# Turning the delta rule's v and output on VectorE and through DRAM instead of on TensorE

## The chip, the cores and the metric

The program runs on one core of one Trainium2 chip. The metric is the device time of that core in microseconds: the median of several executions, and beside it one execution that was taken with the hardware profiler. The names of the engines are those of the profile: PE is TensorE's matrix multiply and PEld its weight load, DVE is VectorE, ACT is ScalarE, POOL is GpSimd, SP is SyncE.

## The reference

One decoder layer on 256 tokens of width 2048. Branch A, which the change touches, is a gated delta rule with 8 heads of width 128, worked in chunks of 64 tokens; branch B is attention; a gated feed-forward layer follows. Cut to branch A:

```python
qkv = silu(causal_dwconv(qkv, conv_w))             # width 4, per channel
q, k = l2norm(q), l2norm(k)                        # v is not normed
t_mat = triangular_solve(eye + a_mat, eye)         # per head and chunk of 64
u = t_mat @ (v * beta)
w = t_mat @ (kb * exp(gc))
def step(state, ...):                              # over the 4 chunks
    v_new = u_n - w_n @ state
    o = qg_n @ state + qk_n @ v_new
    state = state * gl_n + kd_n.T @ v_new
o = rms_norm(o, norm_w) * silu(z)                  # per token and head, over the 128 channels
```

The input projection gives all of its results with channels as rows and tokens as columns. The delta rule needs v the other way round (tokens of a chunk as rows), and its output has to be turned back (channels as rows) for the projection behind it. These two turns are what the change is about.

## The kernel before, in words

All matrix products with weights run on PE with tokens as columns. Each float32 weight block of 1 MB is fetched by SP into one of four buffers, split into a high part (ACT, line 110) and a low part (DVE, line 107), and multiplied in three passes of 128x256 (line 100, through `main_mm`). A block takes two splits of 128x1024 on each of ACT and DVE, and 48 matmuls; high and low parts have two buffers each. A `chunk` (line 181) is two such blocks that fill one of three PSUM buffers, and `join` (line 198) scales it into SBUF and so frees the buffer.

The order of the work: four groups (two heads each) of the chunks q, k, v and z come first, then four groups of the attention's q and k with two long v products, then 16 gate chunks, the branch projections, the output projection, the feed-forward layer. Beside this stream of weight products the small work of the delta rule is written as a Python generator, `gdn` (line 441), one for each group. `main_mm` counts a cost for each matmul and at 1700, that is after 16 matmuls of 128x256, calls `tick`, which moves each open generator forward to its next `yield`. A group of four chunks is 24 ticks; a generator has 51 ticks, so the next two generators begin while it still runs (24 and 48 ticks later).

That order is only a priority. The instructions of every engine are put into their queues by a scheduler at build time: it simulates the program, and an instruction goes out when its engine is free, its data is there and its tile has a place, the one traced earliest first. Instructions can thus run far ahead of the place at which they were written. Each queue is then fixed, and each engine works through its queue in order, waiting where data is late.

A tile belongs to a pool and has a tag (its name, if none is given). All tiles of a tag share `bufs` places. In pool `g`, which the delta rule uses, most have `bufs=1`: `kq` (q and k after the convolution, for PE), `un` (the joined chunk that the convolution reads), `kqh` and `kql` (the high and low parts of `kq`, line 461), `sqq` and `so` (squares, both with tag `sq`, lines 444 and 612), `v`, `vt`, `X`, `E`, `u`, `ot`. A new tile of a tag takes the place once all readers and writers of the former tile in that place are done.

What a generator does, in its order: squares of q; Gram products `g0`, `g1` (lines 467 to 471) from `kqh` and `kql`; norms and decays into `st`, `rt2`, `aq0`, `aq1`; v turned by four PE transposes into PSUM and scaled by `rt2` on DVE into `vb` (lines 496 to 502); the blocks of the triangular matrix sent through DRAM by POOL (`dA`, `dC`, `Xa`); after ten ticks, 15 steps of substitution on DVE (`X`); more DRAM trips on POOL's queue (`dX`, `dE`, `E`, `UB`); from tick 34 on small PE products (`py`, `pu`, `w0`, `z0`, `w1`, `r1`), which read `vb`; the output `po` in PSUM. Then ACT copies `po` to `ot` (line 611) and squares it with a row sum (line 614), a root and a reciprocal give `st[:, 7]`, DVE scales `ot` (line 618), and after seven ticks four PE transposes (line 623) turn it into PSUM, from where DVE multiplies it into `ya` (line 625). The small PSUM tiles of all this share five places (`sdt`).

v's convolution (`conv4`, line 412) writes its result over a rearranged view, so that a head pair of one chunk is one 128x128 block (line 643).

The `g` pool is closed in the third attention group (line 741), and the gate tile `gts` of the next pool takes over its memory.

Of the kernel before, what the change touches and what calls it, by code (L numbers as in the profile page):

```python
# [19 lines left out]
P = 128  # L20
# [52 lines left out]
def layer_kernel(ctx: ExitStack, tc: tile.TileContext, xT, pos, cst, vec, convw, ffw, bdv,  # L73
# [8 lines left out]
    def r3(t, b):  # L82
        return t.rearrange("p (a b) -> p a b", b=b)
# [87 lines left out]
    def sdt(name):  # L171
        return pst[1].tile([P, 512], F32, name=name, tag="sd")
# [239 lines left out]
    def conv4(t, ps, b0, to=None):  # L412
        un = g.tile([P, 2, T], F32, name="un", bufs=1)
        join(un, ps, R1b)
        for j in range(2):
            w = cwv[:, b0 + j, :]
            act.activation(t[:, j, :], un[:, j, :], AF.Identity, scale=w[:, 3:4])
            for d in (1, 2, 3):
                dve.scalar_tensor_tensor(t[:, j, d:], un[:, j, :T - d], w[:, 3 - d:4 - d], t[:, j, d:],
                                         op0=ALU.mult, op1=ALU.add)  # L420
        if to is None:
            act.activation(t, t, AF.Silu)
        else:
            act.activation(to, t.rearrange("p j (b c) -> p j b c", c=64), AF.Silu)
# [12 lines left out]
    def wait(n):  # L437
        for _ in range(n):
            yield

    def gdn(h0, kq, v):
# [54 lines left out]
        pvt = r3(sdt("pvt"), P)  # L496
        for i in range(2):
            for b in range(2):
                pe.transpose(pvt[:, 2 * i + b, :], v[:, 2 * i + b, :], ident)
        vb = g.tile([P, 2, 2, P], F32, name="vb")  # L500
        dve.tensor_tensor(vb, pvt.rearrange("p (i b) d -> p i b d", b=2), rt2[:, :, :, None].to_broadcast([P, 2, 2, P]),
                          op=ALU.mult)
# [10 lines left out]
        pool.tensor_copy(X, C["rows"])  # L513
        yield from wait(10)
# [3 lines left out]
        for i in range(1, 16):  # L518
            tm = g.tile([P, 2, 2, 16], F32, name="tm", tag="tm", bufs=1)
            dve.tensor_tensor(tm[:, :, :, :i + 1], Xd[:, :, :, :i + 1],  # L520
                              Ad[:, :, None, :i + 1, i].to_broadcast([P, 2, 2, i + 1]), op=ALU.mult)
            dve.tensor_reduce(Xd[:, :, :, i], tm[:, :, :, :i + 1], axis=AX.X, op=ALU.add, negate=True)
            if i % 4 == 3:
                yield
        X0, Xm, X1 = Xd[:, 0, :, :16], r3(X[:, :64], 32)[:, :, 16:], Xd[:, 1, :, :16]
# [84 lines left out]
        ot = g.tile([P, 4, P], F32, name="ot", bufs=1)  # L610
        act.copy(ot, po)
        so = g.tile([P, 4, P], F32, name="so", tag="sq", bufs=1)
        for p in range(4):
            act.activation(so[:, p], ot[:, p], AF.Square, accum_out=st[:, 4, p:p + 1])
# [3 lines left out]
        dve.tensor_tensor(ot, ot, st[:, 7, :, None].to_broadcast([P, 4, P]), op=ALU.mult)  # L618
        yield from wait(7)
        pot = r3(sdt("pot"), T)  # L620
        for i in range(2):
            for j in range(2):
                pe.transpose(pot[:, j, i * P:(i + 1) * P], ot[:, 2 * i + j, :], ident)
        yv = ya[:, h0:h0 + 2, :]
        dve.scalar_tensor_tensor(yv, pot, gnv, yv, op0=ALU.mult, op1=ALU.mult)
# [4 lines left out]
    for gr in range(4):  # L630
        h0 = 2 * gr
        kq = g.tile([P, 2, 2, T], F32, name="kq", bufs=1)
        v = g.tile([P, 4, 2 * 64], F32, name="v", bufs=1)
        vt = g.tile([P, 2, T], F32, name="vt", bufs=1)
        for a, t in enumerate((kq[:, 1], kq[:, 0], vt)):
# [4 lines left out]
            if a < 2:  # L640
                conv4(t, ps, 8 * a + h0)
            else:
                conv4(t, ps, 8 * a + h0,
                      v.rearrange("p b (j c) -> p j b c", c=64))
# [320 lines left out]
```

## Time and profile before

| what | value |
|---|---|
| time, median of 3 runs | 1455.61 us (1451.09 to 1455.78) |
| the profiled execution's own time | 1450.71 us |
| its span, first to last instruction | 1448.9 us |
| mean granted TensorE clock | 0.998 |
| busy PE, DVE, ACT, POOL | 1437.9, 951.5, 741.1, 158.1 us |

The delta rule runs from 49.7 us (the first squares of q, line 445) to 355.6 us (the last product into `ya`, line 625). Busy shares over the whole span say little about it, since more than two thirds of the span have other work; the stretches of it are read one by one in the prediction. A busy PE is not a PE at its peak, as the ends of matmuls are modelled: the number of matmuls that start in a stretch is the better measure.

### The profile page before, as it was taken

To read this page: it belongs to the slowest core of one execution; us is meant where nothing else is said; L and a number is where in the kernel's file an instruction comes from. 1 tells how busy PE (TensorE), PEld (TensorE's weight loads), DVE (VectorE), ACT (ScalarE), POOL (GpSimd) and SP (SyncE) were. 2 spreads that over 40 slices of the span, in tenths; PEclk is the share of its full clock that TensorE was granted. 3 is DMA by queue.
4 is the path that set the end of the run, shared out by engine and by line. 5 is a ranking of instruction groups with operands and counts; after the bars stand their busy time and mean duration, and the time that the engine had idled before them with its cause. 6 is when DMAs were issued, how large, how long until landed. Compare 5 with 4: busy or idle time off the path is not lost.

```text
span 1448.9 us, 26704 instructions
## 1 busy us (share of the span) xinstructions
PE 1437.9 (99%) x11232; PEld 1381.6 (95%) x11232; DVE 951.5 (66%) x1389; ACT 741.1 (51%) x1052; POOL 158.1 (11%) x237
## 2 busy tenths in 40 slices
PE   9999999999999999999999999999999999999997
PEld 8999999999999999999999999999999998888886
DVE  7889887765654546767776666666666666555454
ACT  5675774446553444444554545445455455444444
POOL 0024133230030000101120000000000000000000
PEclk9999999999999999999999999999999999999999
DMA  9466656545455555566585555555555555555552
GB/s 342 150 204 211 202 183 210 191 162 173 161 196 180 201 195 187 201 213 226 202 268 197 201 183 199 202 182 199 195 188 200 195 187 202 189 189 203 187 191 88
DMA packets 47465, 283.79 MB, mean 196 GB/s; under 512 B 7744, under 2 KB 8912, under 8 KB 15216
## 3 DMA queue, kind: packets, MB, share of 16 engines
q1 hardware_dynamic: 40352, 270.37, 53.7%
q0 software_dynamic: 6272, 9.61, 2.6%
q8 instruction: 88, 1.44, 0.4%
q10 hardware_dynamic: 720, 2.10, 0.4%
q14 instruction: 33, 0.27, 0.1%
HBM read 275.33 MB, written 3.82 MB: 193 GB/s over the span
## 4 chain that ended last, share of the span: by engine, by line
PE 95%; ACT 2%; DMA 1%; DVE 1%; issue 0%; SPq 0%; ACTq 0%
PE ps_up L100 33%; PE pd L88 17%; PE ps_gate L100 12%; PE ps_gdn L100 7%; PE ps_moba L100 6%; PE ps_wo L100 6%; PE ps_br L100 6%; PE ps_v L100 3%; PE ps_z L100 2%; DMA wraw<-in_w_gdn 1%; PE g L88 1%; DVE wl L107 0%; ACT wh L110 0%; PE ps_bd L88 0%; PE po L88 0%
## 5 line engine op out<-in xcount | busy, mean ns | idle before, releaser
L107 DVE TENSOR_TENSOR wl<-wraw,wh 128x1024 fp32r<-128x1024 f32 (+1 forms) x500 | 598.9, 1235 | 185.8 <-ACT wh L110 185.2
L110 ACT CAST wh<-wraw 128x1024 fp32r<-128x1024 f32 (+1 forms) x500 | 496.6, 1041 | 416.0 <-PE ps_up L100 160.4
L100 PE MATMUL ps_up<-h,wh 128*128 128x256 f32 x2816 | 479.3, 276 | 0.0
L100 PEld LDWEIGHTS ps_up<-h,wh 128*128 128x128 f32 x2816 | 424.1, 188 | 0.1
L100 PE MATMUL ps_up<-h,wl 128*128 128x256 f32 x1408 | 388.7, 276 | 0.0
L100 PEld LDWEIGHTS ps_up<-h,wl 128*128 128x128 f32 x1408 | 264.3, 188 | 0.0
L100 PE MATMUL ps_gate<-hc,wh 128*128 128x256 f32 x1024 | 175.7, 277 | 0.0
L100 PEld LDWEIGHTS ps_gate<-hc,wh 128*128 128x128 f32 x1024 | 154.5, 188 | 0.0
L100 PE MATMUL ps_gate<-hc,wl 128*128 128x256 f32 x512 | 141.8, 277 | 0.0
L88 PE MATMUL pd<-wl,ah 128*128 128x512 f32 x336 | 129.5, 389 | 0.0
L88 PE MATMUL pd<-wh,al 128*128 128x512 f32 x336 | 129.1, 389 | 0.0
L100 PE MATMUL ps_gdn<-hc,wh 128*128 128x256 f32 x704 | 124.7, 280 | 0.0
L100 PEld LDWEIGHTS ps_gdn<-hc,wh 128*128 128x128 f32 x704 | 107.3, 188 | 0.3 <-ACT wh L110 0.3
L100 PE MATMUL ps_gdn<-hc,wl 128*128 128x256 f32 x352 | 98.2, 279 | 0.8 <-DVE wl L107 0.8
L100 PEld LDWEIGHTS ps_gate<-hc,wl 128*128 128x128 f32 x512 | 96.1, 188 | 0.1
L100 PE MATMUL ps_moba<-hc,wh 128*128 128x256 f32 x512 | 92.4, 281 | 0.0
L88 PE MATMUL pd<-wh,ah 128*128 128x512 f32 x336 | 92.1, 389 | 0.0
L200 DVE TENSOR_TENSOR unf<-ps_up,R 128x512 f32<-128x512 f32 x44 | 30.4, 692 | 89.2 <-PE ps_up L100 89.2
L100 PE MATMUL ps_wo<-mc,wh 128*128 128x256 f32 x512 | 87.1, 276 | 0.0
L839 POOL TENSOR_TENSOR acts<-sg,cvf 128x256 f32<-128x256 f32 x44 | 32.4, 737 | 439.2 <-ACT sg L838 432.1
L100 PEld LDWEIGHTS ps_moba<-hc,wh 128*128 128x128 f32 x512 | 78.7, 189 | 0.1
L100 PEld LDWEIGHTS ps_wo<-mc,wh 128*128 128x128 f32 x512 | 77.0, 188 | 0.0
(448 smaller groups left out, 1973.0 us busy)
## 6 DMA issues: line engine op xcount, KB each, us to landing
wraw<-in_w_up SPq DMA_DIRECT2D x88, 1024.0 KB, 4.8
wraw<-in_w_dn SPq DMA_DIRECT2D x44, 1024.0 KB, 4.8
wraw<-in_w_gate SPq DMA_DIRECT2D x32, 1024.0 KB, 4.9
wraw<-in_w_gdn SPq DMA_DIRECT2D x30, 1024.0 KB, 5.1
wraw<-in_w_moba SPq DMA_DIRECT2D x16, 1024.0 KB, 5.0
wraw<-in_w_o SPq DMA_DIRECT2D x16, 1024.0 KB, 4.9
wraw<-in_w_mv SPq DMA_DIRECT2D x8, 1024.0 KB, 5.0
wraw<-in_w_ba SPq DMA_DIRECT2D x8, 1024.0 KB, 4.9
```

The source lines that it names most:

```text
L88: pe.matmul(ps, a, b, start=(start and i == 0), stop=(stop and i == n - 1), **kw)
L100: pe.matmul(ps, a, b, start=start, stop=stop, skip_group_check=True)
L107: return (eng or dve).tensor_tensor(lo, src, hi.bitcast(F32), op=ALU.subtract)
L110: act.copy(hi, src)
L200: dve.tensor_tensor(dst, ps, r, op=ALU.mult)
L839: pool.tensor_tensor(acts[:, c, :], sg, t[:, 1, :], op=ALU.mult)
```

## The change

v's turn. v's convolution now writes plain `v` (`[P, 2, T]`). DVE turns each 32x32 block of it in place of the four PE transposes, into `Zv`, which has tag `kqh`. POOL writes `Zv` to a DRAM tile `dV` in four transfers of 32 partitions (512 runs of 128 bytes each, 64 KB), and reads `vb` back in two (64 partitions of 2 KB runs, 128 KB each). The scaling by `rt2` is no longer part of the eviction on DVE: ACT does it in place, in four `mul`s of 128x128, after the substitution.

The output's turn. ACT takes the squares straight from `po` in PSUM (their values go to a `jk` tile, unused), and scales `po` by `st[:, 7]` with four `mul`s into `ot`; the copy and DVE's scaling are gone. One tick later DVE turns 32x32 blocks in two instructions of 128x256 into `Zo` (tag `kqh`), POOL writes `dO` in four transfers of 512 runs of 128 bytes and reads `yT` (tag `kql`, 256 KB in 2 KB runs) back in one. Ten ticks later DVE multiplies `yT` into `ya`. The generator has 55 ticks.

```diff
+    def rows32(z, r):
+        return z[32 * r:32 * r + 32].rearrange("p c x d -> p (c x) d")
...
-        pvt = r3(sdt("pvt"), P)
-        for i in range(2):
-            for b in range(2):
-                pe.transpose(pvt[:, 2 * i + b, :], v[:, 2 * i + b, :], ident)
-        vb = g.tile([P, 2, 2, P], F32, name="vb")
-        dve.tensor_tensor(vb, pvt.rearrange("p (i b) d -> p i b d", b=2), rt2[:, :, :, None].to_broadcast([P, 2, 2, P]),
-                          op=ALU.mult)
+        Zv = g.tile([P, 2, 8, 32], F32, name="Zv", tag="kqh", bufs=1)
+        dve.transpose(Zv.rearrange("p c x d -> p x c d"), v.rearrange("p j (x c t) -> p (j x) c t", c=2, t=32))
...
+        dV = dr.tile([32, 2, 1024], F32, name="dV")
+        for r in range(4):
+            pool.dma_start(dram(dV, 32 * r, (2048, 32), (P, 16), (1, 32)), rows32(Zv, r))
+        vb = g.tile([P, 2, 2, P], F32, name="vb")
+        for j in range(2):
+            pool.dma_start(vb[64 * j:64 * j + 64].rearrange("p i b d -> p (i b d)"),
+                           dram(dV, 512 * j, (1024, 2), (2048, 32), (1, 512)))
         yield from wait(10)
...
+        for i in range(2):
+            for b in range(2):
+                act.mul(vb[:, i, b], vb[:, i, b], rt2[:, i, b:b + 1])
...
-        ot = g.tile([P, 4, P], F32, name="ot", bufs=1)
-        act.copy(ot, po)
-        so = g.tile([P, 4, P], F32, name="so", tag="sq", bufs=1)
+        jk = g.tile([P, P], F32, name="jk", bufs=1)
         for p in range(4):
-            act.activation(so[:, p], ot[:, p], AF.Square, accum_out=st[:, 4, p:p + 1])
+            act.activation(jk, po[:, p], AF.Square, accum_out=st[:, 4, p:p + 1])
...
-        dve.tensor_tensor(ot, ot, st[:, 7, :, None].to_broadcast([P, 4, P]), op=ALU.mult)
-        yield from wait(7)
-        pot = r3(sdt("pot"), T)
+        ot = g.tile([P, 4, P], F32, name="ot", bufs=1)
+        for p in range(4):
+            act.mul(ot[:, p], po[:, p], st[:, 7, p:p + 1])
+        yield
+        Zo = g.tile([P, 4, 4, 32], F32, name="Zo", tag="kqh", bufs=1)
         for i in range(2):
-            for j in range(2):
-                pe.transpose(pot[:, j, i * P:(i + 1) * P], ot[:, 2 * i + j, :], ident)
+            dve.transpose(Zo.rearrange("p r (j i) t -> p i j r t", i=2)[:, i],
+                          ot[:, 2 * i:2 * i + 2].rearrange("p x (r d) -> p x r d", d=32))
+        dO = dr.tile([32, 2048], F32, name="dO")
+        for r in range(4):
+            pool.dma_start(dram(dO, 32 * r, (2048, 32), (P, 16), (1, 32)), rows32(Zo, r))
+        yT = g.tile([P, 2, T], F32, name="yT", tag="kql", bufs=1)
+        pool.dma_start(yT.rearrange("p j t -> p (j t)"), dram(dO, 0, (512, 4), (2048, 32), (1, 512)))
+        yield from wait(10)
         yv = ya[:, h0:h0 + 2, :]
-        dve.scalar_tensor_tensor(yv, pot, gnv, yv, op0=ALU.mult, op1=ALU.mult)
+        dve.scalar_tensor_tensor(yv, yT, gnv, yv, op0=ALU.mult, op1=ALU.mult)
```

More of the change, by code (lines that the diff above doesn't have):

```diff
@@ L410, in decay, with conv4 @@
         dve.tensor_scalar(cols[:, 0:2, :].rearrange("p a b -> p (a b)"), pt[:, :32], -1.0, None, op0=ALU.mult)
-    def conv4(t, ps, b0, to=None):
+    def conv4(t, ps, b0):
         un = g.tile([P, 2, T], F32, name="un", bufs=1)
@@ L420, in conv4 @@
                                          op0=ALU.mult, op1=ALU.add)
[L421 to L424, printed above, removed]
+        act.activation(t, t, AF.Silu)
     dG = dr.tile([16, T], F32, name="dG", bufs=1)
@@ L632, in layer_kernel @@
         kq = g.tile([P, 2, 2, T], F32, name="kq", bufs=1)
-        v = g.tile([P, 4, 2 * 64], F32, name="v", bufs=1)
-        vt = g.tile([P, 2, T], F32, name="vt", bufs=1)
-        for a, t in enumerate((kq[:, 1], kq[:, 0], vt)):
+        v = g.tile([P, 2, T], F32, name="v", bufs=1)
+        for a, t in enumerate((kq[:, 1], kq[:, 0], v)):
             if gr == 0 and a < 2:
@@ L639, in layer_kernel @@
                 ps = chunk(pair(w_gdn, 4 * gr + a), hc, KD, "gdn")
[L640 to L644, printed above, removed]
+            conv4(t, ps, 8 * a + h0)
             if gr == 0 and a == 1:
```

## The prediction, on record before the result

> **What bounds the kernel now.** I read the page first (busy times, then the shares of the chain that ended last), then that chain in order of time, then stretches of 10 us, then the groups of instructions and the transfers that the change touches.
>
> ```profile
> span 1448.9 us, 26704 instructions
> PE 1437.9 (99%) x11232; PEld 1381.6 (95%) x11232; DVE 951.5 (66%) x1389; ACT 741.1 (51%) x1052; POOL 158.1 (11%) x237
> PE 95%; ACT 2%; DMA 1%; DVE 1%; issue 0%; SPq 0%; ACTq 0%
> ```
>
> The chain is PE's for 95% of the span. Modelled ends make a busy PE look full anyway, so I measure its pace by counts. The chain in order of time (start, length, what, how many):
>
> ```profile
> 183.28 0.44 PE pot L623 x4
> 184.51 2.19 PE g L88 x12
> 187.74 0.44 PE pvt L499 x4
> ...
> 212.31 1.14 PE ps_moba L100 x10
> ...
> 368.04 1.86 PE ps_gate L100 x16
> ...
> 449.53 97.98 PE ps_gate L100 x864
> ```
>
> Undisturbed, 864 matmuls of 128x256 take 97.98 us, 113.4 ns each, or 88 in 10 us. The stretches of the delta rule (PE's matmuls stand behind its busy time; then weight loads, DVE, ACT, POOL):
>
> ```profile
> 85.00:95.00 10.00, 9.96 (x88) 9.76 (x86) 8.74 (x20) 9.86 (x17) 4.42 (x7) 1.00 0.50 163
> 95.00:105.00 10.00, 9.75 (x86) 9.55 (x85) 8.83 (x17) 9.38 (x15) 3.19 (x7) 1.00 0.86 276
> 185.00:195.00 10.00, 10.00 (x86) 9.85 (x85) 8.83 (x26) 7.42 (x15) 3.45 (x8) 1.00 0.61 202
> 195.00:205.00 10.00, 10.00 (x89) 10.00 (x88) 8.73 (x12) 9.14 (x15) 5.50 (x9) 1.00 0.57 185
> 205.00:215.00 10.00, 10.00 (x89) 10.00 (x88) 7.79 (x21) 9.15 (x17) 1.74 (x4) 1.00 0.61 177
> 215.00:225.00 10.00, 10.00 (x89) 10.00 (x88) 9.04 (x28) 6.41 (x16) 0.15 (x1) 1.00 0.64 217
> ```
>
> PE starts 86 to 89 matmuls in each: it issues at its own pace even here, with two others nearly full beside it (DVE 78 to 90%, ACT up to 99%). So a matmul taken from PE shortens the kernel by its slot, and anything that makes DVE or ACT late with the weight splits costs time at once.
>
> **The change, part by part.**
>
> *Removed from PE.* Each turn is four transposes in 0.44 us. Two turns in each of four groups: 8 x 0.44 = 3.52 us. All of it lies on the path: **-3.5 us**. Nothing else of PE's goes; this is the whole direct gain, 0.24%.
>
> *DVE and ACT, instruction by instruction.*
>
> ```profile
> L501 DVE TENSOR_TENSOR vb<-pvt,rt 128x512 f32<-128x512 f32 x4 | 2.7, 687 | 0.6 <-ACT rt L482 0.6
> L618 DVE TENSOR_TENSOR ot<-ot,st 128x512 f32<-128x512 f32 x4 | 2.8, 688 | 0.0
> L809 DVE STREAM_TRANSPOSE xt<-xb 128x512 f32<-128x512 f32 x7 | 5.0, 711 | 0.2
> L564 DVE TENSOR_TENSOR Y<-py,ct 128x256 f32<-128x256 f32 x4 | 1.7, 416 | 0.0
> L611 ACT COPY ot<-po 128x512 f32<-128x512 f32 x4 | 2.3, 583 | 3.4 <-PE po L88 3.4
> L614 ACT ACTIVATE so<-ot 128x128 f32<-128x128 f32 x16 | 4.8, 301 | 0.1
> L585 ACT COPY w<-w 128x128 f32<-128x128 f32 x8 | 2.1, 267 | 4.3 <-PE w L583 4.3
> ```
>
> DVE loses L501 and L618 (1.38 us a group) and gains `Zv` (0.71, the L809 shape) and two turns of 128x256 for `Zo`, a form not in the trace: between half of L809's 0.71 (0.36) and L564's 0.42; I take 0.42, since a fixed part does not halve. The sum is +0.17 us a group. L625 reads SBUF in place of PSUM; I leave its 0.75 us. ACT loses the copy (0.58) and gains four `mul`s for `vb` (301 ns each by L614, a pass over SBUF) and four for `ot` (267 by L585, from PSUM): +1.7 us a group. Neither is on the path: in 215 to 225 us ACT has 3.6 us free and DVE 1.0. Without that cover it would cost the 1.9 us a group, 7.5 in all.
>
> *Added transfers and their wait.* Eight writes and three reads a group go into POOL's queue.
>
> ```profile
> L551 POOL DMA_DIRECT2D E<-dE x4 | 3.2, 790 | 3.8 <-DMA dE<-X 3.8
> L554 POOL DMA_DIRECT2D UB<-dE x32 | 17.2, 546 | 2.1 <-DMA Xa<-dC 2.1
> xn<-xt POOLq DMA_DIRECT2D x16, 128.0 KB, 7.4
> dA<-aq POOLq DMA_DIRECT2D x8, 128.0 KB, 2.2
> gam<-dG POOLq DMA_DIRECT2D x4, 256.0 KB, 4.1
> E<-dE POOLq DMA_DIRECT2D x4, 64.0 KB, 2.4
> UB<-dE POOLq DMA_DIRECT2D x32, 8.0 KB, 4.4
> ```
>
> `E` is the nearest to a write of `dV` or `dO`: 64 KB in runs of 128 bytes; 0.79 us to issue, 2.4 to land. So 8 x 0.79 + 3 x 0.55 = 8 us of issuing a group, 32 in all, on an engine that is at most 55% busy in the stretches above. A turn takes 4 x 0.79 + 2.4 to 4.4 (landing, `E` and `UB`) + 0.55 + 2.2 to 4.1 (`dA`, `gam`) = 8.3 to 12.2 us, in place of about 1 us through PE. I take 10. For v that is hidden: `vb` is wanted at tick 37, 30 ticks after `Zv` is written, 54 us at 16 x 113.4 ns. What waits behind it is ACT's queue, if the scaling stands there before the data are in; behind `vb`'s issue on POOL wait `Xa` and the substitution.
>
> [...]
>
> *The places that the new tiles share.* This is the part on which I think the result turns. `Zo` takes `kqh`'s only place and `yT` takes `kql`'s. Traced in order, group 0's `Zo` and `yT` (tick 45) stand ahead of group 2's `kqh` and `kql` (tick 4, which is tick 52 of group 0). How does the scheduler treat a tile that could be written before one traced earlier in the same place? `sq` is such a tag now (`sqq`, `so`):
>
> ```profile
> 134.70 0.64 ACT L422 ACTIVATE kq<-kq 128x512 f32<-128x512 f32 x1
> 144.56 1.06 ACT L110 CAST kqh<-kq 128x1024 fp32r<-128x1024 f32 x1
> 175.25 0.30 ACT L614 ACTIVATE so<-ot 128x128 f32<-128x128 f32 x1
> 175.68 0.64 ACT L445 ACTIVATE sqq<-kq 128x512 f32<-128x512 f32 x1
> 176.34 0.91 ACT L417 ACTIVATE kq<-un,cwv 128x256 f32<-128x256 f32 x2
> ...
> 171.82 0.69 DVE L200 TENSOR_TENSOR un<-ps_gdn,R 128x512 f32<-128x512 f32 x1 [0.45 <-PE ps_gdn L100]
> 180.87 0.68 DVE L618 TENSOR_TENSOR ot<-ot,st 128x512 f32<-128x512 f32 x1
> 184.53 0.74 DVE L625 SCALAR_TENSOR_TENSOR ya<-pot,vc,ya 128x512 f32<-128x512 f32 x1
> 187.43 0.69 DVE L200 TENSOR_TENSOR un<-ps_gdn,R 128x512 f32<-128x512 f32 x1
> ...
> 225.55 0.69 DVE L618 TENSOR_TENSOR ot<-ot,st 128x512 f32<-128x512 f32 x1
> ```
>
> Group 2's q is ready at 135.3, and its `kqh` split runs ahead at 144.56. Its square `sqq`, which needs q alone, goes out only at 175.68, just behind the last `so` of group 0. The nearest reading: places go in the traced order. The next q convolution (L417, 176.34) writes `kq` and follows at once.
>
> So in the changed kernel group 2's `kql` waits for `yT` of group 0. `ot` is scaled at about 182 (ACT's root and casts end there), `Zo` at 183 to 184, plus 10 us: `yT` is in at 194, L625 at 195, `kql` done at 196.5. That is 15.6 us behind L618's 180.87. It delays three things. The Gram products go from 184.5 to about 198. The q convolution of group 3 goes from 176.34 to about 197, and with it `un` is held, so that the join of k moves from 187.43 to about 201. PSUM covers this: k, v and z fill the three buffers in turn, and the first attention chunk needs k's at 212.3 (`ps_moba`), 11 us later than 201.
>
> Not fully covered is work that moves into 195 to 215.
>
> ```profile
> L482 ACT ACT_TABLE_LOAD x4 | 5.1, 1283 | 0.1
> L482 ACT ACTIVATE rt<-st,epst 64x2 f32<-64x2 f32 x16 | 4.7, 295 | 9.7 <-DVE jk L476 9.5
> ```
>
> ACT: two L417 (0.91), `kqh` (1.06), q's SiLU (0.64) and four roots (4 x 0.295), each of these two with a table load of 1.28: 6.4 us, where ACT has 0.86 + 0.85 = 1.7 us free. Traced earlier, this work goes ahead of the weight splits. The excess, 4.7 us, at worst stops PE for as long; at best it runs on into 215 to 225, where 3.6 us are free, and costs nothing. I take **+2 us**, the middle, as two buffers for each split part give some slack. Group 3's same delay falls where no further q waits for `kq`: nothing.
>
> Group 3 waits for group 1's `yT` in the same way (L618 at 225.55, so Gram products at 243, 14 us late), and its own turn adds 10: it ends at 380 in place of 355.6. The gates' tile takes that memory; they begin at 368 and are first joined 96 matmuls (11 us) later, and two more chunks (22 us) fit in PSUM: hidden.
>
> *Sum.* -3.5 + 2 = -1.5 us on the profiled execution, 1450.7 to 1449.2. The median of the runs was 1455.61, 4.9 above that execution (the runs go from 1451.09 to 1455.78): **1454 us**, within what can be told from no change, 0.3% or 4.4 us. Its own range: -3.5 to +1.2 us, 1452 to 1457.
>
> **The rivals.**
>
> *All hidden, and a little more.* The places are given to whoever is ready, or the excess runs on; then the full 3.5 us, and PE also loses its switches and PSUM waits around the eight turns. The stretch 95 to 105 has 86 starts for 88, 0.25 us lost; with 85 to 105 and 185 to 195 as a guide, 0.2 to 0.3 us in each of four groups: -3.5 - 1.1 = -4.6, 1451. For it: POOL and the transfers have room. Against: the `sqq` row.
>
> *Slower: `yT` comes back too late for `kq`.* The mechanism is the same hand-over of the place, but L625 goes out where it was traced (tick 55, against tick 52 of the waiting `kql`), or `dO` stands behind group 1's eight `UB` issues (4.3 us) and its waits. Beyond 11 us of further delay the PSUM cover is gone: k's buffer is not free at 212, and PE stands still. With 15 us of further delay, 8 of them from the traced place (10 ticks of 1.81 us, less the transfers' 10) and 7 from POOL (8 x 0.546 and `E`'s 2.4), PE loses 4 to 5; with the whole excess of 4.7 on ACT: -3.5 + 4.7 + 5 = +6.2, 1462. It decides from `kql` later than 207 us. For it: the tick order, and the 8 us of issuing that POOL gets more in each group. Against: instructions here run as soon as they can, `kqh` 40 us ahead of its place.
>
> *Slower: landings one behind another.* The four writes of a turn land as slowly as `xn`'s sixteen do, 7.4 us each, and in a row: 30 us in place of 4, so `yT` returns 26 us later, 15 beyond the PSUM cover: -3.5 + 4.7 + 15 = +16, 1471. For it: `xn` and `UB` show that many transfers at once land later than one. Against: `E`. [...]
>
> **How the numbers follow.** Forecast (1452 to 1457): 0.45. All hidden: 0.22. `yT` late: 0.28. Landings in a row: 0.05. Time 1454. The range goes down to the second case's better half, 1449, and up over most of the third, 1467; about 0.07 lies below and 0.1 above. Faster by over 0.3% is the second case, some of which stays inside: 0.2. Slower by over 0.3% is the third and fourth: 0.33. Within 0.3%: 0.47.
>
> **What would show it.** Right: no `pvt` and `pot` on PE; in the rows of ACT, group 2's `kqh` after group 0's `dO` transfers, not at 144.6, `kql` right behind a DVE row `ya<-yT`, the next L417 behind both at about 197; starts of PE in 195 to 215 a few short of 88; the gates at 113.4 ns. Wrong: `kqh` of group 2 still near 145 (places by readiness); `dO` landing in over 5 us; PE short of starts in other stretches, where ACT stands behind `vb` or DVE behind `yT`.

## The result and the profile after

| | before | after |
|---|---|---|
| median of the runs | 1452.60 us (1451.08 to 1455.78, 5 runs) | 1462.65 us (1462.32 to 1468.10, 5 runs) |
| ratio | | 1.0070, 95% interval 1.0053 to 1.0087 |
| profiled execution: own time, span | 1450.71, 1448.9 us | 1465.33, 1463.5 us |

The change makes the kernel 10 us slower; the forecast was 1454. Executions of one program differ by several microseconds: those of the kernel before run from 1450.2 to 1458.6 us over all measurements, and its profiled one, 1450.71, is among the shortest. The page of the changed kernel has these rows for the span, the engines and the chain that ended last:

```profile
span 1463.5 us, 26732 instructions
PE 1441.1 (98%) x11200; PEld 1383.5 (95%) x11200; DVE 950.7 (65%) x1393; ACT 748.0 (51%) x1081; POOL 187.5 (13%) x281
PE 83%; DMA 6%; DVE 3%; ACT 3%; issue 3%; POOL 1%; SPq 0%; POOLq 0%; ACTq 0%; DVEq 0%
```

PE has its 32 instructions fewer, 11200 for 11232. But the chain is PE's for 83% of the span and no longer for 95%: DMA has come in with 6%, VectorE and ScalarE with 3% each. The engines are hardly busier than before, so this is waiting, and stretches of 10 us show where (columns as in the prediction: PE, weight loads, DVE, ACT, POOL, then the granted clock, DMA share, GB/s):

```profile
95.00:105.00 10.00, 9.31 (x81) 9.11 (x79) 7.21 (x18) 8.71 (x16) 2.98 (x6) 1.00 0.87 278
105.00:115.00 10.00, 9.08 (x65) 8.99 (x65) 9.68 (x25) 5.91 (x10) 3.09 (x6) 0.83 0.51 169
145.00:155.00 10.00, 7.90 (x67) 7.54 (x67) 7.23 (x11) 7.09 (x15) 7.25 (x13) 1.00 0.63 182
195.00:205.00 10.00, 7.28 (x61) 6.99 (x60) 4.38 (x5) 1.44 (x2) 5.56 (x10) 1.00 0.79 228
205.00:215.00 10.00, 10.00 (x71) 9.61 (x71) 7.49 (x21) 7.76 (x14) 2.83 (x5) 0.83 0.30 96
345.00:355.00 10.00, 6.69 (x58) 6.48 (x57) 4.49 (x6) 2.92 (x3) 5.49 (x10) 1.00 0.41 143
```

One of the same stretches before:

```profile
145.00:155.00 10.00, 10.00 (x88) 10.00 (x88) 7.67 (x14) 8.28 (x17) 3.04 (x7) 1.00 0.89 274
```

Where before has 86 to 91 starts of PE in these stretches, there are 58 to 81. Two of the rows show a second loss: from 105 and from 205 PE counts as busy for 9.1 and 10 of the 10 us, yet starts only 65 and 71, at a granted clock of 0.83. In stretches of 1 us (PE's busy time and starts, then the clock):

```profile
105.00:106.00 1.00, 0.08 (x1) 1.00 0.46 111
...
107.00:108.00 1.00, 1.00 (x6) 0.50 0.00 0
```

PE is short of 1.6 us in 103 to 106, and then runs at half its clock for over 3 us (0.55, 0.50, 0.50 and 0.75 in the four stretches from 106 to 110), which costs nearly as much again, 1.7 us.

I summed both from 75 to 455 us in stretches of 1 us: what PE is short of 1 in each, and what the clock is short of 1 where PE is at least 80% busy. Before has 0.3 us and nothing; the changed kernel 11.7 and 5.1. So 11.4 + 5.1 - 3.5 for the transposes = 13.0 of the 14.6 us between the two spans. The lost time lies at 103 to 110 (1.6 idle and 1.7 of clock), 145 to 153 (2.1), 201 to 209 (2.7 and 1.7), 218 to 284 (1.8) and 351 to 359 (3.3 and 1.7).

What stops PE is seen in the instructions in order of time. ScalarE's:

```profile
101.27 1.26 ACT L529 ACTIVATE vb<-vb,rt 128x128 f32<-128x128 f32 x4
...
103.38 1.99 ACT L110 CAST wh<-wraw 128x1024 fp32r<-128x1024 f32 x2
...
146.67 1.28 ACT L529 ACTIVATE vb<-vb,rt 128x128 f32<-128x128 f32 x4 [5.96 <-DMA vb<-dV]
147.85 1.98 ACT L110 CAST wh<-wraw 128x1024 fp32r<-128x1024 f32 x2
...
205.18 0.91 ACT L417 ACTIVATE kq<-un,cwv 128x256 f32<-128x256 f32 x2 [8.74 <-DVE kql L107]
205.99 1.98 ACT L110 CAST wh<-wraw 128x1024 fp32r<-128x1024 f32 x2
```

Three times the casts of weights (`wh`, L110) stand behind something new: at 101 behind the four scalings of `vb`, at 146 behind scalings that wait 5.96 us for `vb` to land, and at 205 behind a q convolution that waits 8.74 us for `kql`. But PE waits for the casts only at the first place. Its own rows show what it takes up after a stop; the last row is VectorE's:

```profile
104.47 0.50 PE L100 MATMUL ps_z<-hc,wh 128*128 128x256 f32 x2 [0.69 <-ACT wh L110]
...
147.19 0.60 PE L567 MATMUL py<-Et,S 128*128 128x32 f32 x4 [1.41 <-issue]
...
354.63 0.63 PE L567 MATMUL py<-Et,S 128*128 128x32 f32 x4 [3.31 <-DVE Et L563]
...
146.84 0.24 DVE L563 STREAM_TRANSPOSE Et<-E 128x64 f32<-128x64 f32 x1 [3.63 <-DMA E<-dE]
```

The same step of VectorE before, without a wait:

```profile
136.92 0.24 DVE L558 STREAM_TRANSPOSE Et<-E 128x64 f32<-128x64 f32 x1
```

At 147, 204, 283 and 355 PE takes up `py`, a small product that needs `E` back from DRAM by way of `Et`. (The row at 147 names no releaser, but `Et` ends just before it.) These four stops are 8.0 of the 11.7 us. The weights that were cast late, high and low part, account for 1.6 us (104 and 106), and a Gram product that waits for `kql` at 269 for 0.8. VectorE, PE and GpSimd's queue ahead of the stop at 204:

```profile
201.51 0.75 DVE L636 SCALAR_TENSOR_TENSOR ya<-yT,vc,ya 128x512 f32<-128x512 f32 x1 [3.63 <-DMA yT<-dO]
203.73 0.25 DVE L563 STREAM_TRANSPOSE Et<-E 128x64 f32<-128x64 f32 x1 [1.47 <-DMA E<-dE]
203.90 1.18 DVE L107 TENSOR_TENSOR kql<-kq,kqh 128x1024 fp32r<-128x1024 f32 x1
...
204.03 0.63 PE L567 MATMUL py<-Et,S 128*128 128x32 f32 x4 [2.72 <-DVE Et L563]
...
186.22 2.54 POOL L631 DMA_DIRECT2D dO<-Zo  x4 [0.69 <-DVE st L452]
190.65 0.54 POOL L554 DMA_DIRECT2D dE<-X  x1 [1.88 <-DMA dO<-Zo]
191.34 0.73 POOL L633 DMA_DIRECT2D yT<-dO  x1 [0.15 <-issue]
197.65 0.80 POOL L556 DMA_DIRECT2D E<-dE  x1 [5.59 <-DMA dE<-X]
```

Two round trips are woven together on GpSimd's queue. The second half of `dE` is issued behind the landing of `dO`, and `E` waits 5.59 us for the landing of `dE`; `E` reaches VectorE at 203.73, and until then VectorE and, for `py`, PE stand still. The casts that wait for `kql` come at 205.99, when PE has been busy again since 204.

### The profile page after: what moved, and what is told of

Its sections match the earlier page's. It is cut to its first block, busy times and chain, and to the rows that moved or that the text cites. A ratio compares the mean times of both kernels' runs of the same rounds, so it can differ in the third digit from the quotient of the medians.

```text
span 1463.5 us, 26732 instructions
## 1 busy us (share of the span) xinstructions
PE 1441.1 (98%) x11200; PEld 1383.5 (95%) x11200; DVE 950.7 (65%) x1393; ACT 748.0 (51%) x1081; POOL 187.5 (13%) x281
## 4 chain that ended last, share of the span: by engine, by line
PE 83%; DMA 6%; DVE 3%; ACT 3%; issue 3%; POOL 1%; SPq 0%; POOLq 0%; ACTq 0%; DVEq 0%
PE ps_up L100 33%; PE pd L88 16%; PE ps_gate L100 11%; PE ps_wo L100 6%; PE ps_br L100 6%; PE ps_gdn L100 4%; PE ps_moba L100 3%; PE ps_z L100 2%; DVE wl L107 1%; DMA E<-dE 1%; DMA wraw<-in_w_gdn 1%; ACT wh L110 1%; DMA yT<-dO 1%; DMA dV<-Zv 1%; DMA vb<-dV 1%
## 5 line engine op out<-in xcount | busy, mean ns | idle before, releaser
L110 ACT CAST wh<-wraw 128x1024 fp32r<-128x1024 f32 (+1 forms) x500 | 496.1, 1040 | 403.3 <-PE ps_up L100 160.9
```

Of the source, the lines that this page charges most:

```text
L110: act.copy(hi, src)
```

## The experiments

One table holds all kernels: idle is PE's idle time from 75 to 455 us above the 0.3 us of before, clock is what the half clock costs there, both summed as above; edit is what the kernel takes from PE or adds to it at 0.11 us a transpose; the last column is the profiled span less the 1448.9 us of before.

| kernel | median us | ratio [95%] | idle | clock | edit | sum | span |
|---|---|---|---|---|---|---|---|
| changed | 1462.65 | 1.0070 [1.0053, 1.0087] | 11.4 | 5.1 | -3.5 | 13.0 | 14.6 |
| v_only | 1466.16 | 1.0068 [1.0053, 1.0083] | 11.2 | 4.6 | -1.8 | 14.0 | 15.5 |
| o_only | 1461.82 | 1.0043 [1.0026, 1.0059] | 6.7 | 0 | -1.8 | 4.9 | 6.9 |
| own_places | 1452.35 | 0.9987 [0.9973, 1.0001] | 3.8 | 0 | -3.5 | 0.3 | 0.8 |
| own_places_b | 1454.37 | 0.9998 [0.9982, 1.0015] | 4.1 | 0 | -3.5 | 0.6 | 1.0 |
| y_own | 1460.80 | 1.0044 [1.0029, 1.0059] | 9.5 | 3.4 | -3.5 | 9.4 | 11.5 |
| z_own | 1466.82 | 1.0093 [1.0071, 1.0114] | 12.8 | 5.1 | -3.5 | 14.4 | 14.8 |
| o_own | 1452.95 | 0.9997 [0.9983, 1.0012] | 3.4 | 0 | -1.8 | 1.6 | 3.0 |
| act_scale | 1458.80 | 1.0026 [1.0010, 1.0042] | 0.5 | 0 | 0 | 0.5 | 1.5 |
| dve_scale | 1476.78 | 1.0135 [1.0118, 1.0153] | 20.3 | 6.1 | -3.5 | 22.9 | 26.8 |
| late_scale | 1472.74 | 1.0135 [1.0109, 1.0160] | 16.5 | 5.0 | -3.5 | 18.0 | 20.0 |
| v_late | 1461.00 | 1.0052 [1.0034, 1.0070] | 8.1 | 1.7 | -1.8 | 8.0 | 8.7 |
| own_late | 1458.07 | 1.0030 [1.0015, 1.0046] | 10.5 | 2.5 | -3.5 | 9.5 | 10.5 |
| own_dve | 1460.04 | 1.0040 [1.0024, 1.0056] | 8.9 | 3.1 | -3.5 | 8.5 | 12.3 |
| trips_v | 1456.47 | 1.0016 [1.0002, 1.0031] | 4.2 | 0 | 0 | 4.2 | 5.8 |
| own_sp | 1487.24 | 1.0217 [1.0196, 1.0237] | 26.2 | 12.4 | -3.5 | 35.1 | 37.4 |
| after_sp | 1493.77 | 1.0255 [1.0228, 1.0281] | 30.6 | 14.0 | -3.5 | 41.1 | 44.3 |
| twice | 1460.88 | 1.0056 [1.0035, 1.0077] | 7.2 | 5.1 | +3.5 | 15.8 | 15.8 |
| wait11 | 1455.86 | 1.0014 [0.9999, 1.0028] | 3.4 | 0 | 0 | 3.4 | 4.9 |

The sum leaves 0 to 4 us of each difference, mostly 1 to 2. So the loss of every one of these kernels is, but for that, made of stops of PE, the half clock behind some of them, and the transposes, in the one execution that was profiled. That is one of many: `act_scale`'s was the shortest of its ten (1452.15; the others 1457.6 to 1460.0), so its row does not hold what its median lost; `o_only`'s was also the shortest (1457.55 of 4), and `twice`'s the longest (1466.47; the others 1460.1 to 1461.2).

**Each half of the change alone.** `v_only` takes the change's lines for v and keeps PE's transposes of the output; `o_only` the other way round.

```diff
 # v_only, against the changed kernel
-        Zo = g.tile([P, 4, 4, 32], F32, name="Zo", tag="kqh", bufs=1)
...
+            for j in range(2):
+                pe.transpose(pot[:, j, i * P:(i + 1) * P], ot[:, 2 * i + j, :], ident)
 # o_only, against the changed kernel
-        Zv = g.tile([P, 2, 8, 32], F32, name="Zv", tag="kqh", bufs=1)
...
+                pe.transpose(pvt[:, 2 * i + b, :], v[:, 2 * i + b, :], ident)
```

> Only v is turned the new way (Zv, dV, vb, four scalings on ScalarE); the output keeps its PE transposes, its copy and DVE's scaling. Half of the removed PE slots remain removed: -1.8 us. Theory A (the stalls at 103 to 110 and 145 to 153 us of the changed kernel come from v's part: four scalings of 0.385 us stand in ScalarE's queue ahead of the weight casts, and later wait 6 us for vb): both stalls stay, some 3.4 + 2.4 us, and those from 195 us on go: about +4 us against the kernel before. Theory B (the places of kqh and kql): no stall at all without Zo and yT: -1.8 us. Theory C (POOL's round trips get late whatever is added): stalls in front of py stay in part, +4 to +7.

> Only the output is turned the new way (Zo in kqh's place, yT in kql's place, squares and scaling on ScalarE from PSUM); v keeps its PE transposes and DVE's eviction with the scaling. Half of the removed PE slots remain removed: -1.8 us. Theory B (kql of group 2 waits for yT of group 0, and the casts stand behind the q convolution that waits for kql): the stalls at 195 to 225, 265 to 285 and 345 to 365 stay, those before 155 go: +7 to +9 us. Theory A: no stall, -1.8. Theory C: +3 to +6.

Both are slower than before, by 10 and 6 us, and together they are not the sum: 10 us. `v_only` has no output tile in a shared place and still loses 10, half of it at one spot. ScalarE there:

```profile
221.25 1.28 ACT L529 ACTIVATE vb<-vb,rt 128x128 f32<-128x128 f32 x4 [6.41 <-DMA vb<-dV]
222.53 1.28 ACT L458 ACT_TABLE_LOAD   x1
223.83 1.86 ACT L458 ACTIVATE gam<-gam,cols 128x128 f32<-128x128 f32 x6
225.60 1.03 ACT L110 CAST wh<-wraw 128x1024 fp32r<-128x1024 f32 x1
```

ScalarE takes the scalings while `vb` is on its way, and a table load and six exponentials come behind them before the next cast: the weights come at 225.6. PE waits 2.83 us for them, is short of 4.6 us in all in 223 to 230 and then at half clock until 236 (0.50 in each stretch of 1 us from 229 to 235, then 0.65). Here a wait for `vb` does hold up the weights. But this stop is `v_only`'s own: in the changed kernel the scalings of the same group run at 224.00 after a wait of 0.17 us.

**The shared places.** `own_places` gives `Zo` a place of its own and puts `yT` into `u`'s; `y_own` and `z_own` do one of these, `o_own` both on top of `o_only` (`Zo` into `vt`'s).

```diff
-        Zo = g.tile([P, 4, 4, 32], F32, name="Zo", tag="kqh", bufs=1)
+        Zo = g.tile([P, 4, 4, 32], F32, name="Zo", bufs=1)
...
-        yT = g.tile([P, 2, T], F32, name="yT", tag="kql", bufs=1)
+        yT = g.tile([P, 2, T], F32, name="yT", tag="u", bufs=1)
```

> The whole change, but Zo has a place of its own and yT takes the place of u, which is free by then. Theory B: kqh and kql of group 2 run ahead near 145 us again, the stalls from 195 us on go, and +10 us falls to about +2 (v's stalls less the 3.5 us of PE). Theory C (the trips that POOL's queue makes are late by themselves, E and yT above all): py still waits for E at about 200 and 350 us, and +7 or more stays.

> The kernel with places of its own for the output's blocks again, now in five rounds, to tell whether it is faster than before: it was 0.9987 [0.9973, 1.0001]. Expected 0.998 to 0.9995; by the theory that only chance in the schedule made it so, the same program gives the same time again, since the schedule is made when it is built.

> The changed kernel with yT in u's place instead of kql's; Zo stays in kqh's. Theory: kql of the next group waited for ya<-yT (10.8 us of DMA waits) and stopped PE at 201-205; with yT elsewhere kqh still waits for Zo's transfers, which land about 4 us after they are issued and before it is wanted, so nearly all comes back as with both places moved: 1451 to 1456, and no stop of PE at 201-205. Rival (Zo's sharing is what counts): 1459 to 1465.

> The changed kernel with Zo in a place of its own; yT stays in kql's. Theory: kql still waits for ya<-yT, so the stop at 201-205 stays: 1459 to 1465. Rival (Zo's sharing counts): 1451 to 1456.

> The output's part alone (v is still transposed on PE and scaled by VectorE), Zo in vt's place and yT in u's, neither in the next group's kqh or kql. It saves 16 transposes on PE, 1.8 us. Theory that the shared places made the loss of the output's part alone (+6 us): 1450 to 1455, PE idle below 3 us up to 455 us. Rival (yT's landing before VectorE's multiply is enough by itself, 7.2 us of landing): 1457 to 1463, with VectorE's wait for yT ahead of a stop of PE.

With both moved the whole loss is gone; with either alone it is not. The rows of `kqh` and `kql`, with the start of the first and the last, tell why. Changed kernel:

```profile
L110 ACT CAST kqh<-kq x3: 1037/1047/1055, 102.4 to 254.0; 128x1024 fp32r<-128x1024 f32 x3
L107 DVE TENSOR_TENSOR kql<-kq,kqh x3: 1183/1226/1226, 103.5 to 268.1; 128x1024 fp32r<-128x1024 f32 x3
```

`y_own`:

```profile
L110 ACT CAST kqh<-kq x3: 1035/1042/1050, 102.5 to 258.0; 128x1024 fp32r<-128x1024 f32 x3
```

`z_own`:

```profile
L110 ACT CAST kqh<-kq x3: 1038/1045/1047, 102.0 to 234.5; 128x1024 fp32r<-128x1024 f32 x3
L107 DVE TENSOR_TENSOR kql<-kq,kqh x3: 1183/1227/1230, 103.1 to 267.8; 128x1024 fp32r<-128x1024 f32 x3
```

`own_places`:

```profile
L110 ACT CAST kqh<-kq x3: 1035/1036/1050, 102.5 to 205.5; 128x1024 fp32r<-128x1024 f32 x3
L107 DVE TENSOR_TENSOR kql<-kq,kqh x3: 1209/1224/1226, 103.5 to 207.6; 128x1024 fp32r<-128x1024 f32 x3
```

The last `kqh` stands at 205 with both places moved; it or its `kql` comes 50 to 60 us later when either is shared. Either place alone thus keeps a group's Gram products until the output of an earlier group is on its way. That the two chains of small steps then lie on top of each other, with their transfers on one queue, is how the rows read; no run tests that by itself. In `y_own`, where nothing waits for `kql`, PE still stops at 203 for `py`: `Et` stands on VectorE behind `ya<-yT`, which waited 3.92 us for `yT`. The forecast that `y_own` brings nearly all back was wrong; `z_own` came out a little above its range. `o_own` against `o_only` says the same of the output's part: 0.9997 for 1.0043, each against before.

`own_places` at 145 and 195 has PE's pace back (same columns as above):

```profile
145.00:155.00 10.00, 9.58 (x84) 9.42 (x84) 8.35 (x13) 8.01 (x16) 6.67 (x12) 1.00 0.83 274
195.00:205.00 10.00, 10.00 (x91) 10.00 (x90) 9.90 (x16) 7.39 (x11) 4.94 (x8) 1.00 0.83 271
```

What is left, 3.8 us of stops around 104, 137 and 146, eats the 3.5 us of the transposes. In five more rounds it was 0.9998, so it is the same as before, not faster. Since it holds all of v's part, that part has no fixed price of its own: the 10 us of `v_only` are not in it. `Zv` stays in `kqh`'s place in every kernel with v's new turn; what that costs was not tested.

**The scaling.** `act_scale` does this part alone: before, with VectorE's one multiply replaced by four of ScalarE's. `dve_scale` is the changed kernel with the scaling of `vb` back on VectorE, `own_dve` the same on `own_places`. `late_scale`, `v_late` and `own_late` are the changed kernel, `v_only` and `own_places` with the four scalings held until the block before them has reached `UB`.

```diff
 # act_scale, against before
-        dve.tensor_tensor(vb, pvt.rearrange("p (i b) d -> p i b d", b=2), rt2[:, :, :, None].to_broadcast([P, 2, 2, P]),
-                          op=ALU.mult)
+        for i in range(2):
+            for b in range(2):
+                act.mul(vb[:, i, b], pvt[:, 2 * i + b, :], rt2[:, i, b:b + 1])
 # dve_scale, own_dve
-                act.mul(vb[:, i, b], vb[:, i, b], rt2[:, i, b:b + 1])
+        dve.tensor_tensor(vb, vb, rt2[:, :, :, None].to_broadcast([P, 2, 2, P]), op=ALU.mult)
 # late_scale, v_late, own_late
-                act.mul(UB[64 * j:64 * j + 32, :, b, 64 * j + 32:64 * j + 64], pu[o:o + 32], -1.0)
+                ubm = act.mul(UB[64 * j:64 * j + 32, :, b, 64 * j + 32:64 * j + 64], pu[o:o + 32], -1.0)
+        with tc.issue_after(ubm.ins):
+            for i in range(2):
+                for b in range(2):
+                    act.mul(vb[:, i, b], vb[:, i, b], rt2[:, i, b:b + 1])
```

> The kernel before, with the one multiply of VectorE that scales v replaced by four of ScalarE's from PSUM; PE's transposes stay and no transfer is added. Theory that ScalarE's in-order queue is full at 95-115 and 145-155 (98.6% and 93.8% busy before): the four scalings stand ahead of kqh there and PE stops for about 1.6 us per place: +2 to +6, 1455 to 1459. Rival (only landings count): within 0.15% of before.

> The whole change, but vb is scaled by one instruction on VectorE (0.7 us) in place of four on ScalarE (1.5 us). Theory A in its narrow form (the load on ScalarE): the stall at 103 to 110 goes, -3 us against the changed kernel; the wait for vb's landing moves to VectorE's queue. If the wait is what counts and not the load, the time stays as it is, within 2 us.

> Places of their own for the output's blocks, and vb scaled by one instruction of VectorE instead of four of ScalarE. Theory that ScalarE's four scalings make the stops at 103-106 and 144-147: they go, PE idle falls from 4.1 to below 2 us, 1447 to 1451. Rival (the same program in another order stops elsewhere, as with dve_scale, which came out at 1.0135): 1453 to 1477, with new stops at other places behind VectorE's wait for vb.

> The whole change, but the four scalings of vb are put behind the scaling of UB in ScalarE's queue (tick 36, just ahead of their use), so that no weight cast stands behind vb's landing. Theory A (early place in the queue): the lost starts at 95 to 115 and 135 to 155 us, some 6 us, come back, and the shared places keep their cost: +3 to +5 us against the kernel before. If v's loss is the trips' own: no change, +10.

> Only v turned the new way, with the late scaling. Theory A: the stalls at 103, 147 and 221 us of the v-only kernel go, and the slots of 16 transposes remain: -1.8 us, ratio 0.9988. If v's trips hold up POOL's queue and so py: +2 to +6.

> Zo and yT in places of their own (yT in u's) and the late scaling of vb together. If A and B are the whole loss and the 3.5 us of PE are real: -3.5 us, ratio 0.9976, and 88 starts in 10 us all through the delta rule. If trips on POOL's queue still stop PE: 0 to +4 us.

`act_scale`: +0.26% (0.10 to 0.42), about 3.8 us with no transfer added; its 16 scalings are busy for 4.6 us. That is in the forecast range, but the place is not shown: in its profile PE stops only at 93, for 0.8 us. (The 98.6% and 93.8% of that expectation belong to 85 to 95 and 95 to 105; 145 to 155 had 82.8%.) But taking them off ScalarE, or holding them back, gained nothing: four of these five kernels are slower than the ones they start from, and `v_late`, 1.0052 for 1.0068, can't be told from its own. The stop at 146 was not the scaling's: PE waits there for `py`. In `own_late` the scaling no longer stands at 146, and PE stops for `py` all the same, for 6.3 us at 155. Its queue of GpSimd, and VectorE's row behind it:

```profile
146.58 0.55 POOL L551 DMA_DIRECT2D dE<-X  x1
153.34 0.53 POOL L505 DMA_DIRECT2D Xa<-dC  x1 [6.21 <-DMA dC<-dA]
154.16 0.80 POOL L553 DMA_DIRECT2D E<-dE  x1 [0.29 <-DMA dE<-X]
...
161.05 0.24 DVE L560 STREAM_TRANSPOSE Et<-E 128x64 f32<-128x64 f32 x1 [7.30 <-DMA E<-dE]
```

The same step before:

```profile
130.81 0.54 POOL L549 DMA_DIRECT2D dE<-X  x1 [4.81 <-DVE jk L476]
133.13 0.79 POOL L551 DMA_DIRECT2D E<-dE  x1 [1.77 <-DMA dE<-X]
```

Before, `E` follows `dE` after 2.3 us. In `own_late` the next group's `Xa` has come between them, with a wait of 6.21 us for its own round trip, and `E` goes out 7.6 us after `dE`. The stop at 104 did not go either, though the scalings are no longer there: here a join of 0.68 us runs on VectorE between `kql` and the weights, and PE is short of the same 1.6 us. The other four kernels without the scalings there stop for 1.6 us at 104 too. All eleven profiles with this stop have v's new turn, and `act_scale`, `trips_v`, `o_only` and `o_own` do not have it; the scalings are not needed for it, and what makes it in each is not shown.

**The transfers.** `trips_v` is before with v's transfers added, into `u`'s place before `u` is written, read by nobody; PE still transposes. `own_sp` and `after_sp` are `own_places` and the changed kernel with the new transfers on SyncE's queue.

```diff
 # trips_v, against before
+        for r in range(4):
+            pool.dma_start(dram(dV, 32 * r, (2048, 32), (P, 16), (1, 32)), v[32 * r:32 * r + 32].rearrange("p a (c t) -> p (a c) t", t=32))
+        idle = g.tile([P, 2, T], F32, name="idle", tag="u", bufs=1)
+        for j in range(2):
+            pool.dma_start(idle[64 * j:64 * j + 64].rearrange("p j t -> p (j t)"),
+                           dram(dV, 512 * j, (1024, 2), (2048, 32), (1, 512)))
 # own_sp, after_sp
-            pool.dma_start(dram(dV, 32 * r, (2048, 32), (P, 16), (1, 32)), rows32(Zv, r))
+            sp.dma_start(dram(dV, 32 * r, (2048, 32), (P, 16), (1, 32)), rows32(Zv, r))
...
-        pool.dma_start(yT.rearrange("p j t -> p (j t)"), dram(dO, 0, (512, 4), (2048, 32), (1, 512)))
+        sp.dma_start(yT.rearrange("p j t -> p (j t)"), dram(dO, 0, (512, 4), (2048, 32), (1, 512)))
```

> The kernel before, with v's transfers added: v goes to DRAM and comes back into an unused tile (u's place, before u is written) in the same pieces on GpSimd's queue; nobody reads it, and PE still transposes v. No scaling on ScalarE, no wait on vb. Theory Q: these transfers alone hold E, Xr and dA back and cost 3 to 12 us: 1456 to 1466. Rival: only what waits for vb (the scalings on ScalarE) costs; then 1452 to 1456, the same as before within 0.2%.

> The new transfers (v's and the output's, both ways) are issued from SyncE's queue instead of GpSimd's; the output's blocks keep places of their own. Theory Q: what costs is GpSimd's queue, which takes its transfers in order, so that a round trip waiting there for its own landing holds the next one (in the kernel with the later scaling, dE<-X to E<-dE went from 2 us to 6-8 us with Xa<-dC between them, and PE stopped for py). By Q the own-places loss that is left (stalls at 95-115 and 135-155 worth about 4.5 us, against a gain of 3.5) shrinks, GpSimd issues E<-dE at the time of before, and the time is 1446 to 1452. Rival: weights on SyncE's queue are held behind the landing of dV or dO in the same way; casts then wait for wraw and PE stops there: 1456 to 1475. Rival: ScalarE's scaling alone makes the stalls at 95-115 and 135-155; nothing changes: 1450 to 1454.

> The changed kernel, its new transfers issued from SyncE's queue, the shared places as they are. Theory Q: E<-dE and Xr<-dX are again issued within 3 us of the landing before them; the stalls that came from late E, Xr (195-215, 335-355) go, those from ScalarE's scaling (103, 147) and from kql's shared place stay: 1453 to 1459. If the queue is not the cause: 1460 to 1466. If weights are held behind landings on SyncE's queue: above 1466.

`trips_v` costs 0.16% (0.02 to 0.31), 2.3 us: the transfers alone, with nobody waiting for them, are not the loss of `v_only` (9.9 us). That fits both of its forecasts. Adding `act_scale`'s 3.8 and taking off the 1.8 of the transposes gives 4.3; the other 5 or 6 us are in neither. `v_only`'s stop at 223, behind a wait for `vb`, is of that size, but `own_places` waits for `vb` as well and does not lose them, so they are not shown to be the price of that wait. The queue theory's remedy failed: on SyncE's queue the same waits stand in front of the weights. `own_sp`'s waits of that queue:

```profile
SPq L633 <- DMA dO<-Zo: 10.8, 6, 3.7
SPq L514 <- DMA dV<-Zv: 8.5, 8, 5.3
```

That is 19 us in which the queue waits for landings and asks for no weights; the kernel is 33 us slower than `own_places_b`, run beside it.

**Two controls.** `twice` is before with each of the 32 transposes done twice; `wait11` moves the start of the elimination by one step and changes no instruction.

```diff
 # twice
+                for _ in range(2):
                     pe.transpose(pvt[:, 2 * i + b, :], v[:, 2 * i + b, :], ident)
 # wait11
-        yield from wait(10)
+        yield from wait(11)
```

> The kernel before with each of its 32 PE transposes done twice into the same place. If a transpose is worth its slot on PE, +3.5 us, ratio 1.0024. If transposes hide (PE waits for something anyway): 0.

> The kernel before, with the wait ahead of the elimination in each group set to 11 steps instead of 10; the same instructions, in another order. Theory that the order made when the program is built moves stalls about by itself: the time moves by 2 to 8 us either way, most likely up, with PE idle of 2 to 6 us in the first 455 us where before has 0.3. If the kernel before isn't at a lucky order: within 0.15% of before (1451 to 1455).

`twice` was to price the transposes and does not do that cleanly: beside the 3.5 us it has two stops of 3.9 and 3.5 us that before has not. `wait11` has the very instructions of before, and its profile shows stops of 3.1 us in 135 to 155, where PE starts 142 matmuls and before starts 176 without idle time. It was to show what another order does by itself, and it does not: up to 178 us every engine takes its instructions in the same order in both traces, so these stops lie ahead of the first difference. VectorE waits there for a landing. `wait11`, then `own_places` and `own_places_b`, whose two profiles are of one program with every queue in one order:

```profile
132.51 1.06 DVE L533 TENSOR_TENSOR tw<-W,Xr 128x512 f32<-128x512 f32 x1 [5.01 <-DMA Xr<-dX]
...
134.20 1.07 DVE L538 TENSOR_TENSOR tw<-W,Xr 128x512 f32<-128x512 f32 x1 [3.36 <-DMA Xr<-dX]
...
131.12 1.08 DVE L538 TENSOR_TENSOR tw<-W,Xr 128x512 f32<-128x512 f32 x1
```

`own_places` has a stop of 2.0 us at 137 behind this wait; `own_places_b` has neither. Both stops of `twice` stand behind waits for `Xr` too (4.68 and 4.94 us). So stops of 2.0 us (`own_places`) and 3.1 us (`wait11`) came and went with the landing of a transfer, the first in one and the same program. The median of `wait11` is 1.5 us up, an interval that just holds 1: what the order alone does is not shown. So one stop of 2 to 3 us in one profile should not be put down to an edit.

## Why the prediction was wrong

**The step that failed** is the cover. The prediction hides the new transfers and scalings behind the time at which their own results are wanted ("For v that is hidden", "PSUM covers this") and has no term for a trip that was there before and now comes later. In the changed kernel 8.0 of PE's 11.7 us of stops are for `py`, which waits for `E`, and 5.1 us more are half clock after stops; with `Zo` and `yT` in places of their own the net loss is gone. The stops for `py` go with it: 7.3 us in `z_own`, which is as slow, and 0.4 and 1.9 us in the two profiles of `own_places` and `own_places_b`.

**-3.5 us for the transposes: held, as far as shown.** PE has 32 instructions fewer, and in `own_places` 3.8 us of stops less 3.5 give 0.3, against 0.8 measured. No run shows the term alone.

**ACT and DVE, "Neither is on the path": wrong, in its cover.** The scalings of `vb` in the changed kernel:

```profile
L529 ACT ACTIVATE vb<-vb,rt 128x128 f32<-128x128 f32 x16 | 5.1, 390 | 9.3 <-DMA vb<-dV 9.2 <-issue 0.2
```

`Zo`'s turns are right (438 ns for 0.42) and the product into `ya` from `yT` takes L625's 0.75; the scalings overlap, so the busy 5.1 us of `vb`'s and 4.6 us of `ot`'s are 1.28 and 1.15 us a group, for 1.20 and 1.07. The sizes hold to 0.2 us a group. What failed is the cover: "in 215 to 225 us ACT has 3.6 us free". The scalings do not run there. Group 0's run at 101, where the prediction's own row has ACT 9.38 of 10 us busy, group 1's at 146. The prediction said what queues behind an early scaling ("What waits behind it is ACT's queue") and gave it no price. In the changed kernel the late weights behind the scalings at 101 cost 1.6 us and 1.7 us of clock, though kernels without these scalings stop there as long; at 146 the casts are late too, but what PE waits for is `py`. `act_scale`, with the work alone, is 3.8 us slower than before.

**The turn's 10 us: too short.** The transfers of the changed kernel:

```profile
vb<-dV POOLq DMA_DIRECT2D x8, 128.0 KB, 6.7
dO<-Zo POOLq DMA_DIRECT2D x16, 64.0 KB, 2.6
yT<-dO POOLq DMA_DIRECT2D x4, 256.0 KB, 8.9
E<-dE POOLq DMA_DIRECT2D x4, 64.0 KB, 5.7
```

`dO` fits 2.4 to 4.4 (so does `dV`, 4.4); `vb` and `yT` were to land in 2.2 to 4.1 and took 6.7 and 8.9. From the first `dO` at 186.22 to `yT` in use at 201.51 it is 15.3 us. And a transfer that was there before, `E`, went from 2.4 to 5.7 on the median; the prediction moved nothing behind the new ones. Through `Et` and `py` this is the largest term, 8.0 us of stops, and the prediction has it at nothing.

**The shared places: the mechanism right, the price wrong.** `kqh` of group 2 came at 190.88, not at 144.6; `kql` right behind `ya<-yT`; L417 behind both. `kql` was done at 205.1 for 196.5. But the +2 us rested on PSUM: k's buffer is wanted at 212.3, so 11 us of slack. That cover was never reached. `E`, behind `dO` on GpSimd's queue, held `py` and so PE first. The stop at 201 to 209 cost 4.4 us (2.7 and 1.7); it and those at 268 and 351 are gone with both places moved, so they hang on the shared places, though only the one at 269 is a wait for `kql` itself.

**A term that was missing: the clock.** 5.1 of the 16.5 us lost are half clock after stops.

The rival "`yT` comes back too late for `kq`" named 1462 and the same hand-over, but with another bound: it was to decide only from `kql` later than 207, through PSUM. So its number was met by a sum of other terms: about a third of the loss lies at 103 and 146, ahead of the first output tile, and nearly a third is clock (1.7 us of it at 106, counted in both). That the measured time is this rival's 1462 is luck. The signs that the prediction lists behind "Wrong" did name a part of what happened: PE short of starts where ACT stands behind `vb` or DVE behind `yT`. "Landings one behind another" did not happen to the writes (`dO` 2.6 us); it was reads that landed late (`vb` 6.7, `yT` 8.9).

What stays open: how much of the loss of one kernel is its mechanism, how much the order that its program was given, and how much the landings of the one profiled execution. `late_scale` at 1473 and `dve_scale` at 1477, both slower than the changed kernel that they were to mend, are not explained.

## What to carry to other kernels

An instruction on an in-order engine that waits for a round trip costs what stands behind it (in `v_only` the scalings waited 6.41 us for `vb`, and PE 2.83 us for the weights behind them), so a turn through memory is priced by the queue that it enters (casts on ScalarE, other trips on the transfer queue) and not by when its result is wanted; name that queue's next deadline as the cover. Here the largest cost was an old trip, `E`, that came later (8.0 us of stops for `py`), and not a new tile's own wait; it is found by what the engine that sets the pace takes up after each stop, and not by what looks late on its neighbours. A tile put into a place that the next stage needs early ties the two stages together over the whole of its trip (the last `kqh` came at 254.0 in the changed kernel, at 205.5 in `own_places`): give it a place that comes free late. And before a stop of 2 to 3 us is put down to an edit, profile the same program twice: one of these had such a stop, 2.0 us at 137, in one profile and not in the other.

## What the runs showed of the hardware

In the changed kernel PE's granted clock is 1.00 in 368 of the 380 stretches of 1 us from 75 to 455 us, and 0.50 to 0.75 in the twelve behind its stops at 103, 201 and 351. At 103 to 107 PE is short of 1.6 to 1.8 us in eleven of these profiles; in the changed kernel (there in two pieces, 0.69 and 0.92 us), `v_only`, `y_own` and `z_own` it then runs at 0.50 for about 3 us, in the other seven it stays at 1.00 up to 114. The changed kernel's stops of 2.7 us at 201 and 3.3 at 351 and `v_late`'s of 4.1 at 155 have about 3 us of the half clock behind them, `own_late`'s of 6.3 at 155 has nearly 7 from 160 on; `y_own`'s of 2.7 at 330 and `z_own`'s of 2.0 at 201 have none. What decides between them is not shown.

Some landings on GpSimd's queue took longer in the changed kernel, which issues 44 transfers more there: the median of `E`, unchanged, is 2.4 us before and 5.7 after, `dX<-X` and `Xr<-dX` went from 2.4 and 2.3 to 3.9; `UB` did not, 4.4 and 4.3. They also vary from one execution to the next: the same `Xr` held VectorE for 3.36 us in one profile of a program and not in the other.
